# Casting ahead, products further ahead and three phases instead of four in a dense expert layer

## The chip, the cores and the metric

The kernel runs on one core of a Trainium2 chip. A core has five engines that take their instructions in order, each from its own queue: TensorE (PE; the loads of its stationary operand are listed as PEld), VectorE (DVE), ScalarE (ACT), GpSimd (POOL) and SyncE (SP), which here only issues DMAs. They work on SBUF, an on-chip memory of 128 partitions, and PE writes into PSUM. Sixteen DMA engines, which all queues share, move data between SBUF and the device's memory (HBM). The metric is device microseconds of one execution; the time before is the median of three runs.

## The reference

One layer of a decoder block on 512 tokens of width 1024: a mixing part (gated linear attention and windowed attention), then PEER, a retrieval of single-neuron experts. The second half of the time, and the whole change, lie in PEER:

```
def expert_block(args):
    xb, ib, gb = args
    u = expert_u[ib]
    h = jax.nn.gelu(jnp.einsum('lkd,ld->lk', u, xb), approximate=False)
    return jnp.einsum('lk,lkd->ld', gb * h, expert_v[ib])
```

Each token has 8 x 16 = 128 experts out of 16384, with an index `ib` and a gate `gb` for each; `expert_u` and `expert_v` are 16384 x 1024 in float32.

## The kernel before

The tokens are split. For the last 360 (`TD`) the experts are computed **densely**: all 16384, in 128 blocks of 128, with a gate matrix that is zero where an expert wasn't picked. For the first 152 the picked rows of both tables are **gathered**, and each is multiplied and added up on DVE.

*The dense part.* A **U block** b (`h_step`) multiplies 128 rows of expert_u with the tokens: 24 matmuls into a PSUM bank, a Gelu on ACT, a result of 128 x 360. A **V block** (`v_step`) multiplies the gated result with 128 rows of expert_v: 24 matmuls into eight accumulators, which take all of PSUM. So U and V blocks cannot alternate; they run in **phases** (`PHASES`): U of 72 blocks and V of the same 72, then 21 and 21, 21 and 21, 14 and 14. "U1" below is the U stretch of phase 1, and U72 is the U block 72. The result of U stays in SBUF, in the ring (tile `ring`, 21 buffers), until V needs it. In phase 0 blocks 21 to 71 do not fit: they are spilled to HBM (`hs`, from tile `hw`) and loaded back as `hr` in V (`h_load`).

*Float32 by two parts.* Every operand is split into a high part, a cast to the format that PE takes (fp32r), and a low part, the difference; three products replace one. A weight block arrives by DMA in `raw` (512 KB, 3 buffers); ACT casts `whi`, then DVE subtracts for `wlo`. `Stream.get(u)` asks for block u and at that time issues `whi` and `wlo` of block u+2 and the DMA of u+3.

*The gated product.* `w_a(b)` multiplies the result with the gate on DVE (`wr`) and casts it on ACT (`wh`); `w_b(b)` subtracts on DVE (`wl`). In V block b the code runs `w_a(b+2)`, `pump`, `w_b(b+2)`, then `v_step(b)` with its `get`, and `pump` again. `g_load` brings the gates of four blocks (tile `gt`, 720 KB) and is issued when `w_a` reaches the first of the four before. The gate matrix is built during U of phase 0 (`route`, `feed`: one-hot tiles on DVE, small matmuls on PE in between the U blocks, `gbuild`), and written to HBM as `gd`.

*The gather.* 308 steps: 128 u, 26 x, 128 v, 26 y. A u or v step handles 128 tokens, one expert each. The other 24 tokens are laid out five times, so that an x or y step has 120 rows. POOL issues indirect DMAs (tile `rows`, four at a time), DVE does one 128 x 1024 operation a step. `pump()` decides while the program is built how many steps go behind each block: it adds up estimated times of PE, DVE and the DMAs, and puts in steps as long as DVE and DMAs are less than `SLACK` ahead of PE. The order is then fixed.

*Ends of phases.* `sum_phase` moves the eight accumulators to `yT`: ACT copies them in phase 0, DVE adds them after later phases; two at once, as the next U blocks need their banks, the others behind the next blocks.

Of the kernel before, what the change touches and what calls it, by code (L numbers as in the profile page):

```python
# [9 lines left out]
F32 = mybir.dt.float32  # L10
F32R = mybir.dt.float32r
# [4 lines left out]
OP = mybir.AluOpType  # L16
# [23 lines left out]
UNITS = (["skv"] * 4 + ["glr"] + ["sq"] * 8 + ["gr"] * 8 + ["gb"] * 8  # L40
         + GH[0] + GH[1] + ["wb"] * WB[0] + GH[2] + ["wb"] * (WB[1] - WB[0]) + GH[3] + ["wb"] * (8 - WB[1])
         + ["ga"] * NGA + ["wa", "ga"] * (8 - NGA) + ["wa"] * NGA + ["wo"] * 8 + ["wpq"] * 16)


NB = 128
N0 = 72
NRING = 21
NOO = 6
AHEAD = 5
LEAD = 20  # L50
# [1 line left out]
SLACK = 3.0  # L52
DUTY = 0.92
GL = 3
WA = 2
XG = 24
XR = 128 // XG
XS = -(-128 // XR)
# [3 lines left out]
TD = T - TG  # L62
# [2 lines left out]
CQ = CT // 4  # L65


PHASES = [(0, N0)] + [(b, min(b + NRING, NB)) for b in range(N0, NB, NRING)]
DENSE = [(kind, b) for lo, hi in PHASES for kind in "UV" for b in range(lo, hi)]


@with_exitstack
def tile_block(ctx, tc, xT, wst, smalls, wgk2, keysT, uT, vv, u_rows, v_rows, out):
    nc = tc.nc
    ctx.enter_context(tc.manual_schedule())

    P = ctx.enter_context(tc.tile_pool(name="keep", bufs=1, side="left"))
# [9 lines left out]
    def S(n):  # L87
        return sm[:, SM[n][0]:SM[n][1]]
# [10 lines left out]

    class Stream:  # L100
        def __init__(self, nraw, nsp, ahead):
            self.src, self.raw, self.sp = [], {}, {}
            self.nraw, self.nsp, self.ahead = nraw, nsp, ahead
            self.nd = self.ns = 0
            self.lo_eng = lambda u: nc.gpsimd
            self.defer, self.goal = False, 0

        def dmas(self, n):
            while self.nd < min(n, len(self.src)):
                r = P.tile([128, 1024], F32, name=f"raw{self.nd}", tag="raw", bufs=self.nraw)  # L110
                nc.sync.dma_start(r, self.src[self.nd])
                self.raw[self.nd] = r
                self.nd += 1

        def splits(self, n):
            while self.ns < min(n, len(self.src)):
                u = self.ns
                self.dmas(u + 1)
                r = self.raw.pop(u)
                hi = P.tile([128, 1024], F32R, name=f"whi{u}", tag="whi", bufs=self.nsp)  # L120
                lo = P.tile([128, 1024], F32R, name=f"wlo{u}", tag="wlo", bufs=self.nsp)
                nc.scalar.copy(hi, r)  # L122
                self.lo_eng(u).tensor_tensor(lo, r, hi.bitcast(F32), OP.subtract)  # L123
# [88 lines left out]
    for kb in range(KB):  # L212
        g = S("gmix")[:, kb:kb + 1]
# [621 lines left out]
    for d in range(9):  # L835
        if d < 8:
# [5 lines left out]
            g = S("gffn")[:, d:d + 1]  # L842
# [24 lines left out]
    hr, qps = {}, {}  # L867
# [63 lines left out]
    for hp in range(17):  # L931
# [19 lines left out]
        if hp == NXU - 1:  # L951
# [3 lines left out]
            Dn = ctx.enter_context(tc.tile_pool(name="dense", bufs=1, side="right"))  # L955
# [249 lines left out]
    ring, gts, wrs, ws, accs = {}, {}, {}, {}, {}  # L1205
    later = []
# [7 lines left out]
    def spilled(b):  # L1214
        return NRING <= b < N0

    def h_step(b, each=None):
        w = get("U", b)
        bank = PS.tile([128, 512], F32, name="hp", tag=f"M{b % 2}")
        ps = proj(w, XN, n=TD, c0=TG, bank=bank, each=each)  # L1220
        if spilled(b):
            g = Dn.tile([128, TD], F32, name="hw", tag="hw", bufs=3)
        else:
            g = Dn.tile([128, TD], F32, name="ring", tag="ring", bufs=NRING)
            ring[b] = g
        nc.scalar.activation(g, ps[:, :TD], AF.Gelu)
        pe[0] += 24 * (TD / 2400 + 0.014)
        if spilled(b):
            nc.scalar.dma_start(hs[b - NRING], g)
            xfer(0.5)  # L1230
        for f in later[:2]:
            f()
        del later[:2]

    def h_load(b):
        if spilled(b):
            ring[b] = Lt.tile([128, TD], F32, name="hr", tag="hr", bufs=4)
            nc.sync.dma_start(ring[b], hs[b - NRING])
            xfer(0.5)

    def g_load(q):
        g = Lt.tile([128, NCK, 4 * CT], F32, name="gt", tag="gt", bufs=2)
        nc.sync.dma_start(g, gd[q])
        xfer(1.8)
        gts[q] = g

    def w_a(b):
        if b % 4 == 0 and b // 4 + 1 < NB // 4:
            g_load(b // 4 + 1)
        g = gts[b // 4].rearrange("p c (i t) -> p c i t", t=CT)[:, :, b % 4, :]  # L1250
        wr = Lt.tile([128, TD], F32, name="wr", tag="wr", bufs=2)
        nc.vector.tensor_tensor(wr.rearrange("p (c t) -> p c t", t=CT),  # L1252
                                ring.pop(b).rearrange("p (c t) -> p c t", t=CT), g, OP.mult)
        dve[0] += (2 * TD + 200) / 960
        hi = Lt.tile([128, TD], F32R, name="wh", tag="wh", bufs=3)
        nc.scalar.copy(hi, wr)  # L1256
        wrs[b] = (wr, hi)

    def w_b(b):
        wr, hi = wrs.pop(b)  # L1260
        lo = Lt.tile([128, TD], F32R, name="wl", tag="wl", bufs=3)
        nc.vector.tensor_tensor(lo, wr, hi.bitcast(F32), OP.subtract)  # L1262
        ws[b] = (hi, lo)

# [35 lines left out]
    def pump():  # L1300
        for x in (dve, dma):
            x[0] = max(x[0], pe[0] - SLACK)
        while side and dve[0] < pe[0] + SLACK and dma[0] < pe[0] + SLACK:
            step()

    def sum_phase(ph):
        def f(c):
            if ph:
                nc.vector.tensor_tensor(yT[:, c], yT[:, c], accs[c][:, 0:TD], OP.add)  # L1309
# [27 lines left out]
    BANKS = ("S2", "S2", "PT", "O", "M2", "M3", "M0", "M1")  # L1337
    for ph, (b0, b1) in enumerate(PHASES):
        for b in range(b0, b1):
            if b == b1 - 1:  # L1340
                for v in range(b0, b0 + WA):
                    w_a(v)
                    w_b(v)
            h_step(b, feed if LEAD <= b < N0 - TAIL else None)
            if b == RS[0]:
                dve[0] = 27.0
            for _ in range(RS.count(b)):
                next(r_)
            if b == RS[-1]:
                side.append(gather())  # L1350
            if b == N0 - TAIL - 1:
                for _ in r_:
                    pass
                late[0] = True
                step(4)
                assert early[0] == 0
                sR.close()
                Lt = ctx.enter_context(tc.tile_pool(name="late", bufs=1, side="right"))
                yT = Lt.tile([128, 8, TD], F32, name="yT")
            if b == N0 - GL:  # L1360
                g_load(0)
            if b >= RS[-1]:
                pump()
        while later:
            later.pop(0)()
        big = PS.tile([128, 2, 512], F32, name="oacc", tag="S2")
        for c, tg in enumerate(BANKS):
            accs[c] = big[:, c] if c < 2 else PS.tile([128, 512], F32, name="oa", tag=tg)
        end = b1 == NB
        for b in range(b0, b1 - 2 if end else b1):  # L1370
            h_load(b + WA + 3)
            if b + WA < b1:
                w_a(b + WA)
                pump()
                w_b(b + WA)
            v_step(b, b == b0, b == b1 - 1)
            pump()
            if b == NB - 6:
                flush()
                xr = Dn.tile([128, 4, D], F32, name="xr", tag="gbuf", bufs=2)  # L1380
                nc.sync.dma_start(xr[0:TB, 1], x1s[XG:, 1])
                nc.sync.dma_start(xr[0:XG, 0], x1s[0:XG, 1])
                nc.sync.dma_start(xr[:, 2:4], x1s[:, 2:4])
        if not end:
            sum_phase(ph)
# [92 lines left out]
```

## Time and profile before

| | |
|---|---|
| median of 3 runs | 1954.98 us (1952.24 to 1958.17) |
| the profiled execution | 1948.18 us |
| its span, first to last instruction | 1946.4 us |
| PE busy | 1791.0 us (92%) |
| DVE busy | 1399.3 us (72%) |
| ACT busy | 740.9 us (38%) |
| POOL busy | 686.2 us (35%) |
| DMA, mean over the span | 217 GB/s |

The profile is of one execution. In groups and timelines a row names line, engine, operation, written and read tiles and shapes; in brackets or behind the bar stands how long the engine was idle before and whose work ended that. "ACT whi L122" is ACT's instruction on line 122 that writes `whi`. A matmul's duration overlaps the next one's, so PE's time is read from starts. In windows, PEclk is the granted share of PE's full clock, and the DMA share can pass 1 slightly, as transfers on one engine overlap.

### The profile page before, as it was taken

The page shows a single profiled execution, that of the slowest core. Times are in us where ns is not written, and L with a number is a line of the kernel's source. Part 1 is how long each engine was busy: PE and PEld are TensorE (multiplying, and loading weights), DVE is VectorE, ACT ScalarE, POOL GpSimd, SP SyncE. Part 2 cuts the span into 40 slices and gives each one's busy share as a digit, 9 for nine tenths or more (in the row PEclk, how much of TensorE's full clock was granted, in tenths as well). Part 3 has the DMA queues.
Part 4 walks back from the last instruction along what each step waited for, and adds up shares of the span by engine and source line. Part 5 has one row for each costly group of instructions (what it writes and reads, how often), then busy time and mean ns, then how long its engine had stood idle before and what let it go on. Part 6 is the DMA issues. An engine that isn't in the chain of part 4 may idle for free.

```text
span 1946.4 us, 27062 instructions
## 1 busy us (share of the span) xinstructions
PE 1791.0 (92%) x10087; PEld 1615.4 (83%) x10087; DVE 1399.3 (72%) x2772; ACT 740.9 (38%) x1139; POOL 686.2 (35%) x492
## 2 busy tenths in 40 slices
PE   7999999999989998999998988988989879987977
PEld 5676688887868898999998888888888779976976
DVE  7557524452469967999994877777768789888666
ACT  4445423443442244666663233333323223322322
POOL 2333444445544501112331333232444335534430
PEclk9999999999989999999999999999989999999999
DMA  4221222222432335798999788888999889978995
GB/s 154 76 65 47 63 91 83 71 72 96 152 108 76 98 109 167 234 285 285 321 330 329 286 321 307 308 323 313 271 262 401 288 303 348 362 274 321 266 258 150
DMA packets 159971, 422.24 MB, mean 217 GB/s; under 512 B 15111, under 2 KB 69255, under 8 KB 159455
## 3 DMA queue, kind: packets, MB, share of 16 engines
q1 hardware_dynamic: 108143, 251.31, 38.7%
q0 software_dynamic: 44352, 159.80, 24.1%
q10 hardware_dynamic: 7344, 9.40, 1.4%
q8 instruction: 79, 1.29, 0.3%
q14 instruction: 53, 0.43, 0.1%
HBM read 383.24 MB, written 37.19 MB: 216 GB/s over the span
## 4 chain that ended last, share of the span: by engine, by line
PE 45%; DVE 23%; DMA 11%; issue 10%; ACT 7%; POOL 3%; SPq 1%; ACTq 0%; DVEq 0%; POOLq 0%
PE hp L172 16%; PE mm L172 16%; ACT whi L122 5%; DVE accv L1194 4%; DVE wlo L123 4%; PE mm L189 4%; PE gp L1076 4%; DMA raw<-in_vv_dram 4%; DVE rows L1181 3%; DMA rows<-in_v_rows_dram,misc 3%; POOL rows L1173 2%; DVE wr L1252 2%; DMA raw<-in_uT_dram 2%; DMA rows<-in_u_rows_dram,misc 2%; DVE accy L1194 1%
## 5 line engine op out<-in xcount | busy, mean ns | idle before, releaser
L122 ACT CAST whi<-raw 128x1024 fp32r<-128x1024 f32 x349 | 364.5, 1045 | 207.5 <-DMA raw<-in_uT_dram 108.6
L123 DVE TENSOR_TENSOR wlo<-raw,whi 128x1024 fp32r<-128x1024 f32 x250 | 306.6, 1226 | 120.8 <-ACT whi L122 115.3
L172 PE MATMUL hp<-xh,whi 128*128 128x360 f32 x1024 | 349.8, 342 | 19.3 <-DVE yT L1309 10.5
L172 PE MATMUL hp<-xh,wlo 128*128 128x360 f32 x1024 | 342.6, 335 | 20.7 <-DVE wlo L123 19.0
L172 PE MATMUL hp<-xl,whi 128*128 128x360 f32 x1024 | 340.9, 333 | 0.0
L123 POOL TENSOR_TENSOR wlo<-raw,whi 128x1024 fp32r<-128x1024 f32 x99 | 244.6, 2474 | 244.5 <-ACT whi L122 243.1
L1271 PE MATMUL oa<-wh,wlo 128*128 128x360 f32 x768 | 260.4, 339 | 43.9 <-DVE wlo L123 43.4
L1271 PE MATMUL oa<-wh,whi 128*128 128x360 f32 x768 | 256.4, 334 | 23.6 <-ACT whi L122 21.9
L1173 POOL DMA_INDIRECT rows<-in_v_rows_dram,misc x154 | 183.3, 1190 | 260.2 <-DVE accv L1194 179.5
L1271 PE MATMUL oa<-wl,whi 128*128 128x360 f32 x768 | 250.3, 326 | 0.0
L1173 POOL DMA_INDIRECT rows<-in_u_rows_dram,misc x110 | 134.4, 1222 | 292.1 <-DVE rows L1181 252.2
L1256 ACT CAST wh<-wr 128x360 fp32r<-128x360 f32 x128 | 63.2, 494 | 410.1 <-DVE wr L1252 400.4
L172 PEld LDWEIGHTS hp<-xh,wlo 128*128 128x128 f32 x1024 | 197.1, 192 | 24.5 <-DVE wlo L123 22.6
L172 PEld LDWEIGHTS hp<-xh,whi 128*128 128x128 f32 x1024 | 197.4, 193 | 21.0 <-issue 6.5
L1271 PEld LDWEIGHTS oa<-wh,wlo 128*128 128x128 f32 x768 | 144.4, 188 | 72.0 <-DVE wlo L123 71.4
L172 PEld LDWEIGHTS hp<-xl,whi 128*128 128x128 f32 x1024 | 197.6, 193 | 0.0
L1271 PEld LDWEIGHTS oa<-wh,whi 128*128 128x128 f32 x768 | 144.6, 188 | 38.9 <-ACT whi L122 35.2
L1194 DVE SCALAR_TENSOR_TENSOR accv<-rows,misc,accv 128x1024 f32<-128x1024 f32 x128 | 164.2, 1283 | 4.6 <-DMA rows<-in_v_rows_dram,misc 2.7
L1173 POOL DMA_INDIRECT row<-in_u_rows_dram,misc x44 | 66.7, 1517 | 264.9 <-DVE row L1181 190.9
L1271 PEld LDWEIGHTS oa<-wl,whi 128*128 128x128 f32 x768 | 144.7, 188 | 0.0
L1077 ACT COPY gbuild<-gp 128x512 f32<-128x512 f32 x90 | 99.6, 1106 | 82.5 <-PE gp L1076 81.2
L1262 DVE TENSOR_TENSOR wl<-wr,wh 128x360 fp32r<-128x360 f32 x128 | 69.5, 543 | 83.3 <-ACT wh L1256 79.5
(566 smaller groups left out, 3484.6 us busy)
## 6 DMA issues: line engine op xcount, KB each, us to landing
raw<-in_uT_dram SPq DMA_DIRECT2D x128, 512.0 KB
raw<-in_vv_dram SPq DMA_DIRECT2D x128, 512.0 KB
raw<-in_wst_dram SPq DMA_DIRECT2D x93, 512.0 KB
gd<-gbuild SPq DMA_DIRECT2D x80, 288.0 KB
gt<-gd SPq DMA_DIRECT2D x32, 720.0 KB
hs<-hw ACTq DMA_DIRECT2D x51, 180.0 KB
hr<-hs SPq DMA_DIRECT2D x51, 180.0 KB
rows<-in_v_rows_dram,misc POOLq DMA_INDIRECT x154
```

The lines of the kernel that those rows point to most:

```text
L122: nc.scalar.copy(hi, r)
L123: self.lo_eng(u).tensor_tensor(lo, r, hi.bitcast(F32), OP.subtract)
L172: nc.tensor.matmul(ps[:, :n], a[:, kb, :], b[:, kb, c0:c0 + n], start=(kb == 0 and i == 0), stop=(kb == KB - 1 and i == 2))
L189: nc.tensor.matmul(banks[t], a[:, kb, t * 128:(t + 1) * 128], b[:, k, :], start=(first and k == 0 and i == 0), stop=(last and k == kk - 1 ...
L1076: nc.tensor.matmul(p[:, k], o[:, 0, k], o[:, 1, k], start=True, stop=True)
L1077: nc.scalar.copy(gbs[c].rearrange("p i t -> p t i")[:, q * 4:q * 4 + 4, :], p)
L1173: nc.gpsimd.indirect_dma_start(out=rows[n][0:m, :], out_offset=None, in_=u_rows if kn in "ux" else v_rows, in_offset=bass.IndirectOffsetOn ...
L1181: nc.vector.scalar_tensor_tensor(cur, cur, 1.0, x_[0:m, :], OP.mult, OP.mult, accum_out=h_[0:m, s_:s_ + 1])
L1194: nc.vector.scalar_tensor_tensor(acc[0:m, :], cur, w_[0:m, s_:s_ + 1], acc[0:m, :], OP.mult, OP.add)
L1256: nc.scalar.copy(hi, wr)
L1262: nc.vector.tensor_tensor(lo, wr, hi.bitcast(F32), OP.subtract)
L1271: nc.tensor.matmul(accs[c][:, 0:TD], v_[:, cs], a, start=(first and i == 0), stop=(last and i == 2))
```

## The change

The stream of weights now casts `whi` one block further ahead than it subtracts `wlo` (`his`, `more`), with a fourth buffer of `raw` and `whi`. `wr` is made three blocks ahead (`WA`) and its `wl` one block later; the first three are made together at the end of each U stretch. `g_load` is issued one block later, with the first two before V of phase 0. Phase 0 has 82 blocks, then 23 and 23; the ring has 15 buffers and `hr` 8, and U blocks of later phases that do not fit the ring use `hr`. So blocks 15 to 81 are spilled. `sum_phase` lets ACT copy out the first two accumulators and DVE adds them later.

```
-N0 = 72
-NRING = 21
+N0 = 82
+NRING = 15
+NHR = 8
-WA = 2
+WA = 3
-PHASES = [(0, N0)] + [(b, min(b + NRING, NB)) for b in range(N0, NB, NRING)]
+PHASES = [(0, N0)] + [(b, min(b + NRING + NHR, NB)) for b in range(N0, NB, NRING + NHR)]
...
+        def tile(self, tag, dt, u, n):
+            k = u - len(UNITS)
+            if k >= 0 and k % (n + 1) == n:
+                return Dn.tile([128, 1024], dt, name=f"{tag}{u}", tag=tag + "x", bufs=1)
+            return P.tile([128, 1024], dt, name=f"{tag}{u}", tag=tag, bufs=n)
...
+        def his(self, n):
+            while self.nh < min(n, len(self.src)):
+                u = self.nh
+                self.dmas(u + 1)
+                hi = self.tile("whi", F32R, u, self.nsp)
+                nc.scalar.copy(hi, self.raw[u])
+                self.hi[u] = hi
+                self.nh += 1
...
-                self.dmas(u + 1)
-                r = self.raw.pop(u)
-                hi = P.tile([128, 1024], F32R, name=f"whi{u}", tag="whi", bufs=self.nsp)
+                self.his(u + 1)
+                r, hi = self.raw.pop(u), self.hi.pop(u)
                 lo = P.tile([128, 1024], F32R, name=f"wlo{u}", tag="wlo", bufs=self.nsp)
-                nc.scalar.copy(hi, r)
...
             self.splits(u + 1 if self.defer else self.goal)
-            self.dmas(u + self.nraw + 1)
+            if self.more:
+                self.his(self.goal + self.more)
+            self.dmas(u + self.nraw + self.more + 1)
...
+        elif b < N0 or (b - N0) % (NRING + NHR) < NRING:
+            g = ring[b] = Dn.tile([128, TD], F32, name="ring", tag="ring", bufs=NRING)
         else:
-            g = Dn.tile([128, TD], F32, name="ring", tag="ring", bufs=NRING)
-            ring[b] = g
+            g = ring[b] = Lt.tile([128, TD], F32, name="hr", tag="hr", bufs=NHR)
...
-        if b % 4 == 0 and b // 4 + 1 < NB // 4:
+        if b % 4 == 1 and 4 < b and b // 4 + 1 < NB // 4:
             g_load(b // 4 + 1)
...
-    st.lo_eng = lo_eng
+    st.lo_eng, st.more = lo_eng, 1
...
+        for c in (7, 6):
             if ph:
+                t = Lt.tile([128, TD], F32, name="ev", tag="wr", bufs=3)
+                nc.scalar.copy(t, accs[c][:, 0:TD])
+                later.append(lambda c=c, t=t: add(c, t))
...
             if b == b1 - 1:
                 for v in range(b0, b0 + WA):
                     w_a(v)
+                for v in range(b0, b0 + WA - 1):
                     w_b(v)
...
             if b == N0 - GL:
                 g_load(0)
+                g_load(1)
...
-            h_load(b + WA + 3)
+            if not ph:
+                h_load(b + NHR - 1)
             if b + WA < b1:
                 w_a(b + WA)
-                pump()
-                w_b(b + WA)
+            pump()
+            if b + WA - 1 < b1:
+                w_b(b + WA - 1)
```

The buffers of `wr`, `wh` and `wl` go from 2, 3 and 3 to 3, 5 and 4.

The order of instructions in V of phase 0, about its block 24, first on DVE before. Numbers in names tell buffers of one name apart; `wlo191` is the low part of the 191st weight block of the program.

```order
L1252 TENSOR_TENSOR wr_10319<-hr_10193,gt_10076 128x360
L1262 TENSOR_TENSOR wl_10323<-wr_10319,wh_10321 128x360
L123 TENSOR_TENSOR wlo191_10328<-raw191_10285,whi191_10327 128x1024
L1181 SCALAR_TENSOR_TENSOR rows_10068,misc_4266<-rows_10068,xtok_3904 128x1024
L1252 TENSOR_TENSOR wr_10358<-hr_10237,gt_10076 128x360
```

On ACT before, at the same place:

```order
L1256 CAST wh_10321<-wr_10319 128x360
L122 CAST whi191_10327<-raw191_10285 128x1024
L1256 CAST wh_10360<-wr_10358 128x360
L122 CAST whi192_10366<-raw192_10325 128x1024
L1256 CAST wh_10407<-wr_10405 128x360
```

DVE now:

```order
L1270 TENSOR_TENSOR wr_10749<-hr_10584,gt_10506 128x360
L1280 TENSOR_TENSOR wl_10753<-wr_10710,wh_10712 128x360
L138 TENSOR_TENSOR wlo201_10755<-raw201_10682,whi201_10718 128x1024
L1198 SCALAR_TENSOR_TENSOR rows_10498,misc_4266<-rows_10498,xtok_3904 128x1024
L1198 SCALAR_TENSOR_TENSOR rows_10661,misc_4266<-rows_10661,xtok_3904 128x1024
L1270 TENSOR_TENSOR wr_10794<-hr_10623,gt_10670 128x360
```

ACT now:

```order
L1274 CAST wh_10712<-wr_10710 128x360
L128 CAST whi201_10718<-raw201_10682 128x1024
L1274 CAST wh_10751<-wr_10749 128x360
L128 CAST whi202_10757<-raw202_10720 128x1024
L1274 CAST wh_10796<-wr_10794 128x360
```

Before, `wl_10323` reads `wh_10321`, which reads the `wr_10319` just made; now `wl_10753` reads `wh_10712` of the block before, and `wlo201` a `whi201` that stands ahead of the next `wh` on ACT.

The 120-row steps of the gather (x, which read `xtk`) on DVE before stand among U blocks of phase 1:

```order
L123 TENSOR_TENSOR wlo_12428<-raw_12390,whi_12427 128x1024
L1181 SCALAR_TENSOR_TENSOR rows,misc<-rows,xtk_3905 120x1024
L123 TENSOR_TENSOR wlo_12462<-raw_12425,whi_12461 128x1024
L1181 SCALAR_TENSOR_TENSOR rows,misc<-rows,xtk_3905 120x1024 x2
L123 TENSOR_TENSOR wlo_12502<-raw_12459,whi_12501 128x1024
```

and now among the V blocks 55 to 77 of phase 0:

```order
L1198 SCALAR_TENSOR_TENSOR rows,misc<-rows,xtk_3905 120x1024 x2
L1270 TENSOR_TENSOR wr<-hr,gt 128x360
L1280 TENSOR_TENSOR wl<-wr,wh 128x360
L138 TENSOR_TENSOR wlo_12068<-raw_11994,whi_12030 128x1024
L1198 SCALAR_TENSOR_TENSOR rows,misc<-rows,xtk_3905 120x1024
```

In the same way the y steps move from U and V of phase 3 to V107 to V122. Counted over the whole order of DVE, gather steps before are 45 in U of phase 0, 86 in its V, then 38, 31, 39, 32, 26 and 11 in the stretches that follow (the last the V of phase 3); now 68, 94, 42, 36, 41 and 27.

More of the change, by code (lines that the diff above doesn't have):

```diff
@@ L101, in __init__ @@
         def __init__(self, nraw, nsp, ahead):
-            self.src, self.raw, self.sp = [], {}, {}
+            self.src, self.raw, self.hi, self.sp = [], {}, {}, {}
             self.nraw, self.nsp, self.ahead = nraw, nsp, ahead
-            self.nd = self.ns = 0
+            self.nd = self.nh = self.ns = 0
             self.lo_eng = lambda u: nc.gpsimd
-            self.defer, self.goal = False, 0
+            self.defer, self.goal, self.more = False, 0, 0
+        def tile(self, tag, dt, u, n):
[3 more added lines that the diff above has]
+            return P.tile([128, 1024], dt, name=f"{tag}{u}", tag=tag, bufs=n)
         def dmas(self, n):
             while self.nd < min(n, len(self.src)):
-                r = P.tile([128, 1024], F32, name=f"raw{self.nd}", tag="raw", bufs=self.nraw)
+                r = self.tile("raw", F32, self.nd, self.nraw)
                 nc.sync.dma_start(r, self.src[self.nd])
@@ L1236, in h_load @@
         if spilled(b):
-            ring[b] = Lt.tile([128, TD], F32, name="hr", tag="hr", bufs=4)
+            ring[b] = Lt.tile([128, TD], F32, name="hr", tag="hr", bufs=NHR)
             nc.sync.dma_start(ring[b], hs[b - NRING])
@@ L1247, in w_a @@
     def w_a(b):
-        if b % 4 == 0 and b // 4 + 1 < NB // 4:
+        if b % 4 == 1 and 4 < b and b // 4 + 1 < NB // 4:
             g_load(b // 4 + 1)
         g = gts[b // 4].rearrange("p c (i t) -> p c i t", t=CT)[:, :, b % 4, :]
-        wr = Lt.tile([128, TD], F32, name="wr", tag="wr", bufs=2)
+        wr = Lt.tile([128, TD], F32, name="wr", tag="wr", bufs=3)
         nc.vector.tensor_tensor(wr.rearrange("p (c t) -> p c t", t=CT),
@@ L1254, in w_a @@
         dve[0] += (2 * TD + 200) / 960
-        hi = Lt.tile([128, TD], F32R, name="wh", tag="wh", bufs=3)
+        hi = Lt.tile([128, TD], F32R, name="wh", tag="wh", bufs=5)
         nc.scalar.copy(hi, wr)
@@ L1260, in w_b @@
         wr, hi = wrs.pop(b)
-        lo = Lt.tile([128, TD], F32R, name="wl", tag="wl", bufs=3)
+        lo = Lt.tile([128, TD], F32R, name="wl", tag="wl", bufs=4)
         nc.vector.tensor_tensor(lo, wr, hi.bitcast(F32), OP.subtract)
@@ L1306, in sum_phase, with add @@
     def sum_phase(ph):
-        def f(c):
+        def add(c, src):
+            nc.vector.tensor_tensor(yT[:, c], yT[:, c], src, OP.add)
+            dve[0] += 0.47
+        for c in (7, 6):
             if ph:
-                nc.vector.tensor_tensor(yT[:, c], yT[:, c], accs[c][:, 0:TD], OP.add)
-                dve[0] += 0.47
+                t = Lt.tile([128, TD], F32, name="ev", tag="wr", bufs=3)
+                nc.scalar.copy(t, accs[c][:, 0:TD])
+                later.append(lambda c=c, t=t: add(c, t))
             else:
                 nc.scalar.copy(yT[:, c], accs[c][:, 0:TD])
-        for c in (7, 6):
-            f(c)
-        later.extend([lambda c=c: f(c) for c in range(5, -1, -1)])
+        for c in range(5, -1, -1):
+            a = accs[c][:, 0:TD]
+            later.append(lambda c=c, a=a: add(c, a) if ph else nc.scalar.copy(yT[:, c], a))
     def finish(c):
@@ L1369, in tile_block @@
         end = b1 == NB
+        if not ph:
+            for b in range(NRING, NHR - 1):
+                h_load(b)
         for b in range(b0, b1 - 2 if end else b1):
-            h_load(b + WA + 3)
+            if not ph:
+                h_load(b + NHR - 1)
             if b + WA < b1:
                 w_a(b + WA)
-                pump()
-                w_b(b + WA)
+            pump()
+            if b + WA - 1 < b1:
+                w_b(b + WA - 1)
             v_step(b, b == b0, b == b1 - 1)
```

## The prediction

> **What bounds the kernel now.** The page's first lines give the span and the engines' shares. TensorE (PE) is busy 92% of the span, but that is an average over stages, so the next view is the windows, cut at the stretches of the dense part, which fills the second half.
>
> ```profile
> span 1946.4 us, 27062 instructions
> PE 1791.0 (92%) x10087; PEld 1615.4 (83%) x10087; DVE 1399.3 (72%) x2772; ACT 740.9 (38%) x1139; POOL 686.2 (35%) x492
> ```
>
> In the windows a row gives start and end, length, each engine's busy time, PE's granted clock (PEclk), the share of time that the DMA engines are busy, and what they move.
>
> ```profile
> core 0: us, PE busy (x) PEld busy (x) DVE busy (x) ACT busy (x) POOL busy (x), PEclk, DMA share, GB/s
> 744.00:1022.90 278.90, 274.91 (x1882) 274.28 (x1881) 268.71 (x608) 164.82 (x187) 66.58 (x44) 0.99 0.86 277
> 1022.90:1054.90 32.00, 23.80 (x123) 22.90 (x122) 13.09 (x19) 8.77 (x13) 8.76 (x9) 0.89 1.02 357
> 1054.90:1391.40 336.50, 303.65 (x1731) 280.72 (x1729) 253.40 (x382) 105.52 (x146) 97.63 (x81) 1.00 0.84 305
> 1391.40:1493.60 102.20, 90.11 (x504) 87.38 (x504) 72.72 (x90) 32.02 (x48) 48.10 (x41) 0.95 1.03 307
> 1493.60:1601.90 108.30, 90.17 (x504) 81.84 (x504) 86.94 (x97) 32.39 (x44) 35.38 (x33) 1.00 0.84 311
> 1601.90:1685.90 84.00, 83.97 (x505) 84.00 (x505) 74.98 (x68) 28.84 (x42) 48.12 (x40) 0.98 0.96 359
> 1685.90:1795.10 109.20, 89.69 (x506) 81.80 (x505) 88.81 (x97) 31.21 (x43) 40.93 (x33) 0.99 0.82 297
> 1795.10:1864.80 69.70, 60.50 (x337) 59.61 (x337) 48.19 (x46) 18.02 (x27) 27.73 (x24) 0.92 0.96 274
> 1864.80:1924.90 60.10, 52.82 (x288) 48.68 (x289) 43.47 (x52) 18.46 (x27) 11.23 (x8) 0.96 0.86 236
> 1924.90:1946.40 21.50, 13.95 (x78) 10.56 (x76) 11.71 (x28) 0.89 (x1) 0.00 (x0) 0.95 0.23 74
> ```
>
> The rows from 1022.9 are: the last five U blocks of phase 0 (U67 to U71), its 72 V blocks, 21 U, 21 V, 21 U, 21 V, 14 U, 12 V, and the last two V blocks with the end. A block is 24 matmuls. The row of 1601.9 shows U blocks that never wait: 21 in 84.0 us, 4.00 each. V blocks that never wait stand at the start of the first V stretch, seven of them (x168, a window of line 1271 alone):
>
> ```profile
> 1054.90:1082.44 27.54, 27.54 (x168) 27.54 (x169) 1.00 0.73 251
> ```
>
> That is 3.93 us a block. Yet the 72 V blocks take 336.5, or 4.67 each, and the two later V stretches of 21 blocks 108.3 and 109.2 (5.2 each). PE loses 336.5 - 283 = 53 us in the first and 26 and 27 us in the others. VectorE (DVE) explains it, first by its groups in the stretch 1054.9 to 1391.4:
>
> ```profile
> L1181 DVE SCALAR_TENSOR_TENSOR rows<-rows,xtok 128x1024 f32<-128x1024 f32 x83 | 98.9, 1219 | 0.0
> L123 DVE TENSOR_TENSOR wlo<-raw,whi 128x1024 fp32r<-128x1024 f32 x73 | 89.4, 1225 | 38.6 <-ACT whi L122 37.5 <-PE oacc L1271 0.8 <-issue 0.3
> L1262 DVE TENSOR_TENSOR wl<-wr,wh 128x360 fp32r<-128x360 f32 x71 | 38.5, 543 | 45.0 <-ACT wh L1256 43.7 <-issue 1.3
> ```
>
> and then by the timeline of one V block, on DVE and on ScalarE (ACT):
>
> ```profile
> 1119.41 0.53 DVE L1252 TENSOR_TENSOR wr<-ring,gt 128x360 f32<-128x360 f32 x1
> 1120.58 0.54 DVE L1262 TENSOR_TENSOR wl<-wr,wh 128x360 fp32r<-128x360 f32 x1 [0.64 <-ACT wh L1256]
> 1121.52 1.22 DVE L123 TENSOR_TENSOR wlo<-raw,whi 128x1024 fp32r<-128x1024 f32 x1 [0.41 <-ACT whi L122]
> ...
> 1120.05 0.49 ACT L1256 CAST wh<-wr 128x360 fp32r<-128x360 f32 x1 [4.10 <-DVE wr L1252]
> 1120.45 1.04 ACT L122 CAST whi<-raw 128x1024 fp32r<-128x1024 f32 x1
> ```
>
> DVE makes wr, then waits 0.64 for ACT's wh before wl, then 0.41 for ACT's whi before wlo. ACT has sat idle 4.10 us, for wr: a ring of the two engines, with 1.05 us of DVE idle a block. Over the stretch that is 38.6 + 45.0 = 83.6 us of idle beside 253.4 busy: 337.0, which is the stretch (336.5). **So V stretches are bound by DVE with its waits for ACT, not by PE.**
>
> **The change part by part.**
>
> *Casts and products ahead.* whi is cast three blocks ahead instead of two, wr three instead of two, with wl made one block after its wr. In the changed order both things that DVE waits for belong to the block before; ACT, which idles 4.10 us of every 5.5, has made them by then. The 83.6 us go. What is late next: DVE's own work, PE, or the DMAs. For 82 V blocks DVE's work is 253.4 x 82/72 = 289 us (the order gives 94 gather steps on 82 blocks, 86 on 72 before, so the same mix), PE's is 82 x 3.93 = 322. PE is next, if the DMAs follow.
>
> *The DMAs.* Sizes are in the page's list of DMA issues, rates in windows, and DVE's groups in the windows of 1380 and 1818 tell which gathers run there.
>
> ```profile
> raw<-in_vv_dram SPq DMA_DIRECT2D x128, 512.0 KB
> ...
> gt<-gd SPq DMA_DIRECT2D x32, 720.0 KB
> ...
> hr<-hs SPq DMA_DIRECT2D x51, 180.0 KB
> ```
>
> ```profile
> 1380.00:1460.00 80.00, 69.92 (x386) 67.16 (x385) 53.15 (x75) 25.42 (x40) 35.96 (x29) 0.94 1.03 258
> 1460.00:1500.00 40.00, 35.54 (x207) 34.09 (x207) 34.67 (x35) 13.69 (x20) 20.40 (x19) 1.00 1.02 400
> 1818.00:1908.00 90.00, 75.09 (x415) 70.95 (x414) 61.21 (x62) 24.40 (x36) 29.22 (x24) 0.94 1.00 259
> ```
>
> ```profile
> L1181 DVE SCALAR_TENSOR_TENSOR rows<-rows,xtk 120x1024 f32<-120x1024 f32 x25 | 30.6, 1226 | 23.8 <-DMA rows<-in_u_rows_dram,misc 23.8
> ...
> L1194 DVE SCALAR_TENSOR_TENSOR accy<-rows,misc,accy 120x1024 f32<-120x1024 f32 x23 | 29.5, 1282 | 2.7 <-DMA rows<-in_v_rows_dram,misc 2.4
> ```
>
> Full engines (share about 1) carry 400 GB/s at 1460, but 258 at 1380 and 259 at 1818. The last two rows are DVE's groups in those two stretches: there the gather runs its 120-row steps, x and y. While they are in flight everything is slow. A weight or a gather of 128 rows is 0.524 MB, a gate load 0.737, an hr load 0.184, an x or y gather 0.491.
>
> V0 to V54 of the changed phase 0 need 55 weights, 14 gate loads, 47 hr and 60 gathers: 28.8 + 10.3 + 8.6 + 31.5 = 79 MB, 198 us at 400 GB/s and 258 at the 307 that this kind of stretch shows now; PE needs 216. I take 223, near PE, because the row of 1460 shows what the engines carry when they are asked. V55 to V77 hold the 26 x steps, which today stand beside U blocks. There 23 weights, 6 gate loads, 20 hr and the x gathers are 12.1 + 4.4 + 3.7 + 12.8 = 33 MB: 90 us if PE sets the time, 128 at 258 GB/s. I take 122, near the row, a little less since some of it falls between x transfers. V78 to V81: 16. **V of phase 0: 361 us.**
>
> The Trainium skill, page "DMA: Bandwidth & Descriptors", in "Why a DMA increments its semaphore by 16 and not by 1", says that a transfer is split over the largest number of engines up to 16 that divides its rows, so 120 rows would use 15. By that rule x would lose a sixteenth, V55 to V77 would be PE's 90 us and the sum some 60 us lower (with y as well); the trace does not agree, since the rate falls by a third, and the sum stays with the trace.
>
> *Phases.* U of phase 0 gets ten blocks more: 10 x 4.00 = 40 us. The gate building beside it is the same work spread thinner; DVE there is at 268.7 of 278.9, and gets ten wlo and 23 gather steps at 1.22, so 309 of 319: tight, 1 us allowed (0 to 10). U77 thus starts at 1064. The five blocks after it cost 32.0 today (20 of work, DMAs at 1.02); with one weight more in store I take 31 (20 to 35). 16 more blocks are spilled and read back, 16 x 2 x 0.184 = 5.9 MB; the writes hide under U, where the DMAs are at 0.86, the reads are counted above.
>
> *U of phases 1 and 2.* 23 blocks, 92 us each. The first loses the x steps, which made it 102.2 for 21; both look like the row of 1601.9, where the order has 39 gather steps on 21 blocks (now 42 and 41 on 23).
>
> *V of phase 1.* DVE without its waits:
>
> ```profile
> L1194 DVE SCALAR_TENSOR_TENSOR accv<-rows,misc,accv 128x1024 f32<-128x1024 f32 x34 | 43.6, 1282 | 0.5
> ```
>
> This is from the stretch 1685.9 to 1795.1: (88.81 - 43.6)/21 = 2.15 us a block beside the gather, so 23 x 2.15 + 36 x 1.28 = 95.6 for the 36 steps of the new order, above PE's 90.4. I take 100 (90 to 119, the old pace).
>
> *First products moved, gate loads a block later, sums by ACT.* U93 waits for DVE to add out the accumulators:
>
> ```profile
> 1601.93 0.40 PE L172 MATMUL hp<-xh,whi 128*128 128x360 f32 x1 [4.17 <-DVE yT L1309]
> ...
> PE hp L172 <- DVE yT L1309: 10.5, 2, 6.3
> ```
>
> Now ACT copies the two that the next U blocks need, so the 4.17 and 6.3 become a copy of about half a microsecond; one of the two boundaries is gone with its phase. The 92 for U2 has that in it. Two gate loads together before V0 fall into the stretch priced at 31.
>
> *V of phase 2 and the end.* It holds all y steps, in V107 to V122: with the rows fetched ahead some 18 blocks, 12.8 + 9.4 + 3.3 = 25.5 MB, at 259 GB/s 98 us against PE's 71. So 21 x 3.93 + 30 = 112 (83 to 120), then the last two blocks and the end as now, 21.5.
>
> **Sum**, from the profiled execution: 1064 + 31 = 1095, + 361 = 1456, + 92 = 1548, + 100 = 1648, + 92 = 1740, + 112 = 1852, + 21.5 = 1873.5. Its own time is 1948.18 for a span of 1946.4, so 1.8 lie around it: 1875, **73 us less**. The median of the runs is 1954.98, 6.8 above the profiled one; less 72 it is **1883**.
>
> **The rivals.**
> - *The DMAs take over in V.* If mixed traffic carries no more than the 305 to 311 GB/s of today's V rows, V0 to V54 take 258 and V of phase 1 (35 MB) 113: 48 us more, 1931. For it: the share is 0.84 already, and the waits removed were DVE's. Against it: 400 at 1460.
> - *The 120-row gathers cost nothing extra*, since their slowness came from U blocks that asked for everything at once: 32 us less for x and 30 for y, 1821. Against it: 259 GB/s in 1818 to 1908, of which half are V blocks.
> - *Slower: x beside V starves DVE.* DVE takes a row step in its place in the order; if the row is late, wr, wl and wlo queue behind it, and PE behind them; already now DVE waits 23.8 us for 25 rows. From 1883 to 1961 it must lose 78 us more; that is when the 33 MB of V55 to V77 take 200 us, below 165 GB/s. It would give 1965. Against it: 258 holds with three quarters of the share on gathers.
> - *It does not do what it says.* If ACT's whi, behind a raw load that lands late, still comes last, the 1.05 us of each V block stay, and only boundaries are won: V of phase 0 at today's 4.67 is 383, with 27 for x 410 against 361, and V of phase 1 at 5.2 is 120 against 100: 69 us more, 1952.
>
> **How the numbers follow.** Forecast 0.62, by its own bounds 1858 to 1905; DMAs bound 0.15; x free 0.07; starving 0.07; nothing removed 0.09. The range 1855 to 1930 leaves out the two last, which end near or above the time before, and the free x, and reaches to the DMA case, whose size is itself an upper one. A measurement of this kernel tells about 0.3% (6 us) from no change: faster 0.87 (the first three and part of the last), same 0.05, slower 0.08.
>
> **What would show it.** In the changed profile wl and wlo of V blocks should have almost no idle for wh or whi; V blocks before the 120-row steps 4.0 to 4.1 us; the V blocks with x about 5.3, with the DMA share at 1 and near 260 GB/s, DVE then waiting for rows; U stretches at 4.0 a block; no wait of U for yT over 1 us. I am wrong if DVE's idle in V goes to rows or raw loads all through phase 0, if U of phase 0 stretches past 1100, or if x and y run at 400 GB/s.

## The result and the profile after

| | before | changed |
|---|---|---|
| median | 1953.61 us (4 runs, 1949.94 to 1958.17) | 1834.54 us (4 runs, 1830.56 to 1837.78) |
| ratio, 95% interval | | 0.9388 [0.936, 0.9417] |
| the profiled execution | 1948.18 us, span 1946.4 | 1830.56 us, span 1828.8 |

The change takes 119 us off, 6.1%. The forecast had 73, and the range, 1855 to 1930, misses the time on the fast side. One run of e1 below, in which the granted clock was 0.846 instead of 0.985, took 1976.41 us and is left out of its median. The page of the changed kernel shows PE at 96% where it was at 92%:

```profile
span 1828.8 us, 27244 instructions
PE 1754.5 (96%) x10087; PEld 1618.4 (88%) x10087; DVE 1377.6 (75%) x2764; ACT 746.6 (41%) x1141; POOL 697.8 (38%) x492
```

The windows of the changed kernel, cut at its own stretches (length, then busy time of PE, PEld, DVE, ACT and POOL, the clock, the DMA share and GB/s): U20 to U76 with the gate building, U77 to U81, V0 to V54, V55 to V77, V78 to V81, U1, V1, U2, and V of phase 2 up to V125. The row of the last two blocks and the end, 20.7 us, is left out.

```profile
744.00:1059.60 315.60, 310.47 (x2098) 310.01 (x2097) 301.78 (x652) 179.20 (x205) 102.72 (x67) 0.99 0.91 305
1059.60:1089.20 29.60, 23.23 (x123) 22.64 (x122) 13.37 (x20) 8.59 (x13) 9.11 (x8) 0.88 0.97 352
1089.20:1306.50 217.30, 217.30 (x1323) 217.30 (x1322) 184.56 (x288) 84.65 (x113) 77.52 (x60) 1.00 0.99 365
1306.50:1412.00 105.50, 96.07 (x553) 91.91 (x552) 71.74 (x112) 31.48 (x43) 24.79 (x22) 0.98 1.04 295
1412.00:1429.70 17.70, 16.81 (x98) 15.70 (x98) 17.36 (x22) 7.36 (x11) 11.85 (x8) 1.00 1.01 402
1429.70:1521.50 91.80, 91.80 (x553) 91.80 (x553) 84.75 (x74) 35.38 (x54) 51.64 (x47) 1.00 1.01 394
1521.50:1612.40 90.90, 90.90 (x554) 90.90 (x553) 89.65 (x101) 33.52 (x46) 42.54 (x35) 1.00 0.98 377
1612.40:1704.20 91.80, 91.80 (x554) 91.80 (x553) 84.74 (x80) 33.32 (x48) 52.50 (x44) 1.00 1.00 373
1704.20:1808.10 103.90, 90.79 (x506) 87.46 (x505) 73.88 (x88) 30.12 (x42) 23.89 (x21) 0.95 0.98 259
```

In V0 to V54, U1, V1 and U2 PE's busy time is the whole stretch: 3.95 us a V block, 3.99 a U block, no wait at all, with the DMA engines at 0.98 to 1.01. What is lost behind U76 lies mainly in three places: V55 to V77 and V of phase 2, where the 120-row gathers run (295 and 259 GB/s), and U77 to U81.

DVE's groups by shape in V0 to V54, and one V block there on DVE and on ACT, the views that carried the argument before:

```profile
L138 DVE TENSOR_TENSOR wlo<-raw,whi 128x1024 fp32r<-128x1024 f32 x56 | 68.6, 1226 | 31.1 <-issue 16.6 <-ACT wh L1274 12.6 <-ACT whi L128 1.9
L1280 DVE TENSOR_TENSOR wl<-wr,wh 128x360 fp32r<-128x360 f32 x56 | 29.3, 524 | 0.0
```

```profile
1187.70 0.53 DVE L1270 TENSOR_TENSOR wr<-hr,gt 128x360 f32<-128x360 f32 x1
1188.15 0.53 DVE L1280 TENSOR_TENSOR wl<-wr,wh 128x360 fp32r<-128x360 f32 x1
1188.59 1.22 DVE L138 TENSOR_TENSOR wlo<-raw,whi 128x1024 fp32r<-128x1024 f32 x1
```

```profile
1188.32 0.49 ACT L1274 CAST wh<-wr 128x360 fp32r<-128x360 f32 x1 [3.17 <-DVE wr L1270]
1188.72 1.04 ACT L128 CAST whi<-raw 128x1024 fp32r<-128x1024 f32 x1
```

wl now starts 0.45 us after wr, before ACT has begun the wh of that wr; it reads the wh of the block before. wl has no idle time at all. wlo still has 31.1 us of idle in this stretch, 0.55 a block: 1.9 is put down to whi, 12.6 to the wh ahead of it, and 16.6 to nothing that the profile shows. As PE never waits here, none of it costs time.

### The profile page after: what moved, and what is told of

The parts are those of the page before. It is cut to its first block, busy times and chain, and to the rows that moved or that the text cites. A ratio compares the mean times of both kernels' runs of the same rounds, so it can differ in the third digit from the quotient of the medians.

```text
span 1828.8 us, 27244 instructions
## 1 busy us (share of the span) xinstructions
PE 1754.5 (96%) x10087; PEld 1618.4 (88%) x10087; DVE 1377.6 (75%) x2764; ACT 746.6 (41%) x1141; POOL 697.8 (38%) x492
## 4 chain that ended last, share of the span: by engine, by line
PE 72%; DMA 11%; DVE 10%; ACT 3%; issue 2%; SPq 1%; POOL 1%; DVEq 0%; ACTq 0%; POOLq 0%
PE hp L189 26%; PE mm L189 17%; PE oa L1289 13%; DMA raw<-in_vv_dram 5%; PE mm L206 4%; PE gp L1093 4%; PE oacc L1289 4%; DMA rows<-in_v_rows_dram,misc 2%; DMA hr<-hs 2%; DMA raw<-in_uT_dram 1%; DVE wlo L138 1%; PE sc L933 1%; ACT whi L128 1%; DVE stt L413 0%; DVE accy L1211 0%
## 5 line engine op out<-in xcount | busy, mean ns | idle before, releaser
L189 PE MATMUL hp<-xh,whi 128*128 128x360 f32 x1024 | 345.7, 338 | 2.0 <-ACT hw L1244 2.0
L189 PE MATMUL hp<-xh,wlo 128*128 128x360 f32 x1024 | 337.3, 329 | 10.1 <-DVE wlo L138 10.1
L1289 PE MATMUL oa<-wh,wlo 128*128 128x360 f32 x768 | 255.3, 332 | 9.6 <-DVE wlo L138 9.2
L1289 PE MATMUL oa<-wl,whi 128*128 128x360 f32 x768 | 254.1, 331 | 7.0 <-DVE wl L1280 7.0
L1190 POOL DMA_INDIRECT row<-in_u_rows_dram,misc x67 | 102.7, 1533 | 268.7 <-DVE row L1198 192.9
L189 PEld LDWEIGHTS hp<-xh,wlo 128*128 128x128 f32 x1024 | 194.0, 189 | 10.8 <-DVE wlo L138 10.7
L189 PEld LDWEIGHTS hp<-xh,whi 128*128 128x128 f32 x1024 | 193.7, 189 | 2.6 <-ACT hw L1244 2.6
L1190 POOL DMA_INDIRECT rows<-in_u_rows_dram,misc x87 | 108.4, 1246 | 224.6 <-DVE rows L1198 188.6
L189 PEld LDWEIGHTS hp<-xl,whi 128*128 128x128 f32 x1024 | 193.8, 189 | 0.0
L189 PE MATMUL mm<-hhi,whi 128*128 128x512 f32 x264 | 107.1, 406 | 0.9 <-DVE gb L587 0.9
```

Source lines behind the costliest of these rows:

```text
L189: nc.tensor.matmul(ps[:, :n], a[:, kb, :], b[:, kb, c0:c0 + n], start=(kb == 0 and i == 0), stop=(kb == KB - 1 and i == 2))
L1190: nc.gpsimd.indirect_dma_start(out=rows[n][0:m, :], out_offset=None, in_=u_rows if kn in "ux" else v_rows, in_offset=bass.IndirectOffsetOn ...
L1289: nc.tensor.matmul(accs[c][:, 0:TD], v_[:, cs], a, start=(first and i == 0), stop=(last and i == 2))
```

## The experiments

The times of before beside these runs are 1949 to 1952 us; each ratio is against them. "The changed kernel" is 1834.5.

**e1, weights not cast ahead.** The fourth buffers of `raw` and `whi` and the step ahead go.

```
-            if k >= 0 and k % (n + 1) == n:
-                return Dn.tile([128, 1024], dt, name=f"{tag}{u}", tag=tag + "x", bufs=1)
...
-    st.lo_eng, st.more = lo_eng, 1
+    st.lo_eng, st.more = lo_eng, 0
```

> The changed kernel with the weight highs cast at the same distance as the lows again (no fourth raw and whi buffer). Theory (the ring between DVE and ACT was the cost, and the cast ahead is what opens it): whi stands on ACT behind the wh that waits for this block's wr, so wlo waits about 1.05 us a V block again; DVE then needs 2.03 + 1.05 + gather, about 4.4 us a V block in phase 0 and 5.0 in phase 1: 50 to 65 us slower than the changed kernel, 1885 to 1900. Rival (the longer phase 0 and fewer phases bring most of the gain): under 20 us slower, below 1855.

1904.1 us, ratio 0.9765 [0.9731, 0.9799]: 70 us slower than the changed kernel, a little more than the theory's range. The window of V0 to V54 and DVE's groups in it:

```profile
1098.29:1340.21 241.92, 227.77 (x1322) 215.89 (x1321) 181.50 (x281) 78.42 (x109) 69.41 (x58) 1.00 0.90 317
```

```profile
L135 DVE TENSOR_TENSOR wlo<-raw,whi 128x1024 fp32r<-128x1024 f32 x55 | 67.4, 1225 | 61.4 <-ACT whi L125 61.4
L1277 DVE TENSOR_TENSOR wl<-wr,wh 128x360 fp32r<-128x360 f32 x54 | 28.4, 526 | 0.0
```

wlo waits for whi 61.4 us in 55 blocks, 1.12 each; 181.5 busy + 61.4 idle is 242.9, the stretch (241.9). Both waits of before have moved to one place and together are about as long as they were (83.6 us in 72 blocks, 1.16 each). The edit also takes away a buffer of `raw`, but no wait of whi for a raw load shows in this stretch, so it is the cast that comes late, and not the load.

**e2, products not ahead.**

```
-WA = 3
+WA = 2
...
-            if b + WA - 1 < b1:
-                w_b(b + WA - 1)
+            if b + WA < b1:
+                w_b(b + WA)
```

(and `w_a`, `w_b` in turn for the first two products of a phase)

> The changed kernel with wr two blocks ahead and wl in the same block as its wr again. Theory: only wl's wait for wh comes back, 0.64 to 0.75 us a V block: phase 0 rises from 3.95 to about 4.1 us a block, phase 1 to about 4.7: 25 to 35 us slower than the changed kernel, 1860 to 1870. Rival (each of the two steps ahead is enough by itself, since PE has two blocks in store): under 6 us.

1851.18 us, ratio 0.9496 [0.9472, 0.9519]: 17 us slower, between theory and rival. V0 to V54:

```profile
1088.69:1305.93 217.24, 217.24 (x1322) 217.24 (x1322) 184.94 (x286) 80.41 (x111) 89.94 (x59) 1.00 0.98 358
```

```profile
L1280 DVE TENSOR_TENSOR wl<-wr,wh 128x360 fp32r<-128x360 f32 x55 | 29.3, 533 | 32.3 <-ACT wh L1274 32.3
```

The wait for wh is back, 0.59 a block, but 184.9 + 32.3 is just PE's own 217.2, so this stretch loses nothing. V1, with 1.6 gather steps a block instead of 1.1, does: 98.9 us instead of 90.9. So do V55 to V81, with 135.5 instead of 123.2; there ACT waits 46.7 us for raw loads ahead of whi, and wl waits 40.2 us for wh.

**e3, neither ahead.** Both edits together.

> Both steps ahead undone, phases, gate loads and sums as in the changed kernel. Theory: V blocks run at the pace of before (4.7 in phase 0, 5.2 in phase 1): 60 to 80 us slower than the changed kernel, 1895 to 1915, with wl and wlo waiting 0.64 and 0.41 us a block. Rival (phases bring it): 1850 or below.

1905.74 us, ratio 0.9783 [0.9758, 0.9809]: 71 us slower, and no slower than e1. V0 to V54 and its groups:

```profile
1095.53:1335.56 240.03, 227.08 (x1322) 215.87 (x1322) 186.83 (x281) 78.76 (x110) 70.92 (x58) 1.00 0.91 319
```

```profile
L135 DVE TENSOR_TENSOR wlo<-raw,whi 128x1024 fp32r<-128x1024 f32 x55 | 67.4, 1225 | 23.0 <-ACT whi L125 22.2 <-PE oacc L1286 0.8
L1277 DVE TENSOR_TENSOR wl<-wr,wh 128x360 fp32r<-128x360 f32 x54 | 28.8, 533 | 30.2 <-ACT wh L1271 30.2
```

186.8 + 53.2 is 240.0, the stretch again. So the product ahead alone is worth nothing that the runs can tell (e1 against e3, 1904.1 and 1905.7): the wait it removes reappears before wlo, since whi follows wh on ACT. The cast ahead alone is worth 55 us (e2 against e3), and the product ahead 17 on top of it.

**e4, x and y gathers of 128 rows.** The indirect DMAs fetch eight rows more, row 0 each time, into partitions that nothing reads.

```
-                    m = 128 if kn in "uv" else XP_
+                    m = 128
                     nc.gpsimd.indirect_dma_start(
```

> The changed kernel, in which the indirect DMAs of the x and y steps fetch 128 rows instead of 120 (the eight more, of row 0, are not used). Theory (the 120-row shape slows every transfer): the DMAs carry about 390 to 400 GB/s in these stretches instead of 260 to 295, V blocks 55 to 77 run at 3.95 (15 us less) and V of phase 2 loses its 20 us: 30 to 35 us faster than the changed kernel, 1800 to 1805. Rival (the stretches are slow by what is fetched or by demand): no change, 1835.

**1795.54 us**, ratio 0.921 [0.9187, 0.9233]: 39 us faster than the changed kernel. V55 to V77 and V of phase 2:

```profile
1311.40:1402.20 90.80, 90.80 (x554) 90.80 (x553) 78.25 (x121) 34.34 (x46) 35.12 (x24) 1.00 0.98 367
1692.50:1775.70 83.20, 83.20 (x507) 83.20 (x506) 75.08 (x89) 29.74 (x42) 22.69 (x21) 1.00 0.85 320
```

105.5 has become 90.8 and 103.9 has become 83.2, with PE busy all the way. The queues from 1311 to 1400, in the changed kernel and then in e4, with packets, MB, and the time that the packets took as a share of the 16 engines' span (q1 carries the loads that SP issues, q0 the gathers):

```profile
q1 hardware_dynamic: 5687, 15.54, 59.7%
q0 software_dynamic: 2894, 9.88, 43.5%
```

```profile
q1 hardware_dynamic: 6981, 20.25, 61.7%
q0 software_dynamic: 3383, 12.29, 36.2%
```

A MB of gathers took half as long again as in e4 (4.4% of that span instead of 2.9%), and a MB of the other loads a quarter longer (3.8% instead of 3.0%): the shape slows what flies beside it too. By the rule in the Trainium skill's page "DMA: Bandwidth & Descriptors", section "Why a DMA increments its semaphore by 16 and not by 1", a transfer of 120 rows would go over 15 engines. As an estimate from that rule, a sixteenth would be lost. The runs do not agree: full engines carry 258 GB/s (before) and 289 (the changed kernel) with such gathers, and 400 and 402 without. Why the shape does this no run shows.

**e5, phases of 72, 23, 23 and 10.** `N0 = 72` in the changed kernel.

> The changed kernel with a phase 0 of 72 blocks, so phases of 72, 23, 23 and 10. Theory (the steps ahead are the gain, phases are worth little once the sums are ACT's): within 15 us of the changed kernel's 1835, so 1825 to 1850. Rival (fewer phases are a large part of the gain): 1860 or more.

1835.26 us, ratio 0.9401 [0.9382, 0.942]: no difference to the changed kernel. In this order x and y stand beside U of phases 1 and 3: all U stretches together take 34 us more than in the changed kernel, all V stretches 30 less.

**e6, sums on DVE.** The first two sums of a later phase by `add(c, accs[c])` at once, without the copy `ev`.

> The changed kernel with the first two accumulators of a later phase added by DVE at once, as before. Only the boundary from V of phase 1 to U of phase 2 has this. Theory (that boundary's 4.2 and 6.3 us were DVE behind its gather steps): U105 waits 3 to 6 us for yT, 4 to 7 us slower with the slower clock after it, 1838 to 1842. Rival (DVE is now early enough by itself): under 2 us.

1837.98 us, ratio 0.9424 [0.9407, 0.944]: 3 us by the medians, with intervals that meet. The wait at U105, expected at 3 to 6 us, is 0.48:

```profile
1620.74 0.40 PE L189 MATMUL hp<-xh,whi 128*128 128x360 f32 x1 [0.48 <-DVE yT L1326]
```

With the ring of waits between DVE and ACT open, DVE reaches the sums nearly when PE needs them, as the rival has it. The expected wait did not come.

**e7, gate loads one block earlier.** `b % 4 == 0` again in `w_a`.

> The changed kernel with the gate load issued at the first of four blocks again, where it waits for the buffer that the block just before frees. Theory (SP has weights in store, so its wait reaches nobody): under 5 us. Rival (SP's queue behind the gate load holds up the weights): V blocks wait for whi once in four, 10 us or more.

1844.23 us, ratio 0.944 [0.9418, 0.9461]: 10 us slower by the medians, twice the theory's limit, though one of its five runs took 1836.03, inside the changed kernel's range. SP's waits from 1089 to 1300, of e7 and then of the changed kernel (L119 issues the weights, L1261 the gates):

```profile
SPq L119 <- DVE wlo L138: 78.0, 38, 3.9
SPq L1261 <- DVE wr L1270: 71.4, 13, 7.7
```

```profile
SPq L119 <- DVE wlo L138: 116.0, 45, 5.1
SPq L1261 <- DVE wr L1270: 14.6, 12, 2.4
```

SP stands 71 us before gate loads, up to 7.7 each, with weights behind. V0 to V54 bear it (217.3 in both). V55 to V81, with x, take 131.0 us by PE's starts instead of 123.2; but e6, which is the changed kernel up to there, takes 127.1, so half of that can be a difference between executions. That the rival is right where the DMA engines are slow is likely, and not shown.

**e8, the kernel before with 128 rows.** The edit of e4.

> The kernel before with x and y fetched as 128 rows. Theory: the slow transfers go there too: U of phase 1 falls from 102 to about 85 us and U of phase 3 from 70 to about 58, the V stretches, which DVE sets, stay: 25 to 30 us faster than before, 1920 to 1925. Rival (the shape only matters beside the loads of V): no change.

1918.65 us, ratio 0.9828 [0.9809, 0.9847]: 33 us faster than before. The U stretches of phases 1 and 3:

```profile
1392.60:1478.00 85.40, 84.15 (x506) 83.85 (x505) 72.14 (x90) 32.60 (x48) 61.54 (x41) 1.00 0.98 374
1783.40:1843.30 59.90, 58.61 (x337) 57.71 (x337) 47.93 (x46) 18.23 (x27) 26.31 (x24) 0.96 0.90 330
```

102.2 and 69.7 have become 85.4 and 59.9. The shape costs beside U as well as beside V.

**e9, neither ahead, and 72, 23, 23 and 10.** e3 with the edit of e5.

> Both steps ahead undone and phases of 72, 23, 23 and 10: of the change only the buffers, gate loads and sums stay. The question is why the kernel with neither step ahead is still 45 us faster than before, while phases alone cost nothing. Theory (where DVE sets V, every gather step that a longer phase 0 puts beside U takes 1.15 us out of V; where PE sets it, nothing): 15 to 30 us slower than 1905, so 1920 to 1935. Rival (phases are worth nothing here either): 1905.

1928.5 us, ratio 0.989 [0.9867, 0.9913]: 23 us slower than e3, where the same edit cost nothing in e5. The time is the theory's, but the stretches show another cause. U of phase 1 (23 blocks) and of phase 3 (ten blocks):

```profile
1372.22:1492.90 120.68, 98.31 (x554) 94.10 (x553) 81.95 (x100) 35.08 (x52) 61.62 (x47) 0.97 1.03 301
1810.94:1868.23 57.29, 42.68 (x241) 40.60 (x240) 38.97 (x40) 13.46 (x20) 24.27 (x20) 0.95 0.99 256
```

By the theory V would be longer than in e3. All V stretches together take 602.9 us against 619.6, 17 less, with nearly as many gather steps beside them (157 against 153). U is longer, 660.4 against 617.8, and that in the two rows above, where x and y now stand: U of phase 1 took 92.0 in e3. So the forecast was met by luck. What the edit moves is the place of the 120-row gathers; in e3 they stand beside V blocks that DVE slows anyway, which would hide a part of what they cost. That reading fits, and was not tested.

**e10, writes of the gate matrix spread.** e4, with the last eight `put`s one a block instead of all at once.

```
-        while gout:
-            gout.pop(0)()
+        gout.pop(0)()
```

(with a `gout.pop(0)()` behind each U block from 77 on and ahead of each V block, while any is left)

> The 128-row kernel with the last eight writes of the gate matrix issued one a block instead of all at once ahead of the weights of U79. Theory (U79 and U80 lose 10 us because their weights stand behind these writes on SP): U79 and U80 fall from 18.5 us together to 8 to 10, 1785 to 1790. Rival (the DMA engines are full there whatever the order): no change, 1795.

**1786.94 us**, ratio 0.9166 [0.9149, 0.9183], the fastest: 9 us below e4. SP's timeline about U79 in e4, where U77 starts at 1063.6, then in e10, where it starts at 1058.9 (L119 loads weights, L1099 writes gates):

```profile
1065.05 9.89 SPq L1099 DMA_DIRECT2D gd<-gbuild  x8
1075.35 1.92 SPq L119 DMA_DIRECT2D raw<-in_uT_dram  x1
1077.37 1.60 SPq L119 DMA_DIRECT2D raw<-in_vv_dram  x2
```

```profile
1060.33 0.36 SPq L1099 DMA_DIRECT2D gd<-gbuild  x1
1060.78 0.45 SPq L119 DMA_DIRECT2D raw<-in_uT_dram  x1
1061.29 0.81 SPq L1099 DMA_DIRECT2D gd<-gbuild  x1
1062.21 0.70 SPq L119 DMA_DIRECT2D raw<-in_vv_dram  x1
```

The weight goes out 1.9 us after the start of U77 instead of 11.7, and U77 to V0 takes 22.9 us by PE's starts where e4 took 30.6. U79 and U80 take 10.8 together instead of 18.5, a little more than the theory's 8 to 10. So the weights stood behind the writes on SP, and the rival fell.

**e11, e9 with the sums of e6.**

> As e9, with the first two sums of later phases on DVE again, so that two boundaries have them. The question is what the 22 us between e9 and before are. Theory (where DVE sets V, the sums stand behind its gather steps, 4.2 and 6.3 us in the trace of before): 6 to 12 us slower than e9, 1935 to 1941. Rival (as with both steps ahead, little): under 4 us.

1932.75 us, ratio 0.9924 [0.9898, 0.9951]: 4 us slower than e9 for two boundaries, nearer to the rival's 4 than to the theory's 6.

**e12, the kernel before with eight hr buffers.** `bufs=8` for `hr`.

> The kernel before with eight hr buffers instead of four, nothing else. In V of phase 0 SP waits 117 us in all for such a buffer, with the weights behind it. Theory (DVE sets that stretch, weights are in store): under 6 us. Rival (late weights are part of the cost): V0 to V71 fall from 336 to under 326, 10 us or more.

1945.11 us, ratio 0.9982 [0.9964, 1.0]: 0 to 7 us less, 4 by the medians, which fits the theory. V of phase 0 takes 329.4 us by PE's starts, 7 less than before, where the rival asked for 10. Of the 22 us between e9 and before, sums and hr buffers thus account for some 8 by the medians; the rest was not divided.

## Why the prediction was right in kind and too small

The mechanism was right: DVE's waits for ACT set the V stretches, they went, and PE came next. The stretches show which terms of the sum were off:

| stretch | forecast, us | measured, us |
|---|---|---|
| start of U77 | 1064 | 1059.6 |
| U77 to U81 | 31 | 29.6 |
| V0 to V54 | 223 | 217.3 |
| V55 to V77, with x | 122 | 105.5 |
| V78 to V81 | 16 | 17.7 |
| U1 | 92 | 91.8 |
| V1 | 100 | 90.9 |
| U2 | 92 | 91.8 |
| V2 up to V125, with y | 112 | 103.9 |
| the last two blocks and the end | 21.5 | 20.7 |
| span | 1873.5 | 1828.8 |

Of the 45 us, 25 are the two stretches with 120-row gathers and 9 are V1; the range ends 28 us below the forecast, so the 25 alone would not have left it, and the 34 do. **The step that failed is the pricing of the 120-row stretches, "V55 to V77 hold the 26 x steps" and "I take 122", and "112" for y: the time of the slow transfers was nearly right, but all of it was booked as the time of these blocks.** The slow stretches of the changed kernel, by the DMA rate:

```profile
1288.00:1408.00 120.00, 110.57 (x643) 106.68 (x641) 82.08 (x128) 36.47 (x50) 31.27 (x27) 0.99 1.03 289
1698.00:1796.00 98.00, 87.00 (x486) 84.22 (x485) 71.06 (x85) 28.50 (x41) 27.75 (x24) 0.95 1.03 269
```

They last 120 and 98 us, and 122 and 98 had been worked out. That is so close partly by luck: the 120 us moved 34.7 MB at 289 GB/s, where the forecast had 33 MB at about 270. But the first begins 18 us before V55, when its rows are fetched ahead, and PE lives on what is in store until V61; the loss is 105.5 - 90.8 = 15 us, not 31. For y I had allowed 18 blocks for rows fetched ahead, and it was about 21: U126 to about V123, with a loss of 21 instead of 30. e4 confirms both from the other side: without the slow shape these stretches take 90.8 and 83.2.

The prediction also expected DVE to wait for rows beside x. DVE's groups in V55 to V77:

```profile
L1198 DVE SCALAR_TENSOR_TENSOR rows<-rows,xtk 120x1024 f32<-120x1024 f32 x24 | 28.6, 1218 | 0.0
L138 DVE TENSOR_TENSOR wlo<-raw,whi 128x1024 fp32r<-128x1024 f32 x22 | 26.9, 1222 | 35.4 <-ACT whi L128 31.0 <-PE oacc L1289 2.6 <-issue 1.8
```

The rows were never late there; the weights were. wlo waited 31.0 us for whi, and from V55 to V81 ACT waited 57.0 us for raw loads. In V of phase 2 DVE did wait for rows of y, 16.5 us.

The next term is V1, 9 us. I took DVE's work from a stretch in which it waited between its instructions. Back to back they overlap, in V1 of the changed kernel:

```profile
1559.85 1.28 DVE L1211 SCALAR_TENSOR_TENSOR accv<-rows,misc,accv 128x1024 f32<-128x1024 f32 x1
1561.05 0.53 DVE L1270 TENSOR_TENSOR wr<-ring,gt 128x360 f32<-128x360 f32 x1
1561.50 0.53 DVE L1280 TENSOR_TENSOR wl<-wr,wh 128x360 fp32r<-128x360 f32 x1
1561.94 1.22 DVE L138 TENSOR_TENSOR wlo<-raw,whi 128x1024 fp32r<-128x1024 f32 x1
1563.08 1.28 DVE L1211 SCALAR_TENSOR_TENSOR accv<-rows,misc,accv 128x1024 f32<-128x1024 f32 x1
```

Each starts some 0.08 us before the one ahead of it ends, so wr, wl and wlo take 2.03 us from start to start, not 2.15, and a gather step 1.20 to 1.25 instead of 1.28. DVE is busy 89.65 of 90.9 there: it just keeps up. That is 5 of the 9 us (95.6 had been worked out); the other 4 are the allowance up to the 100 that was taken. V0 to V54 (6 us) was such an allowance too: 216 had been worked out for PE. The start of U77 (4 us) is no term that was off: e4 and e6, whose programs are the same up to there, reach it at 1063.6 and 1063.4.

Point by point: casts and products ahead, right, but the prediction treated them as one; e1 to e3 show that the cast carries them. The DMAs, right that they carry 365 to 400 GB/s in V when asked, and the rival that they would stop at 305 to 311 fell. The time measured lies nearest to the 1821 of the rival in which x and y cost nothing extra, but that rival fell: 120-row gathers are slow by themselves beside U and beside V, as e4 and e8 show. Phases, right in the sum by accident: the stretches were priced one by one, and e5 shows that 82 or 72 makes no difference to the changed kernel, as what U loses to the 120-row gathers V gains. Sums by ACT, overpriced: with both steps ahead the wait is 0.48 us even on DVE. Gate loads a block later, which the prediction priced at nothing of their own: e7 has about 10 us by the medians. The rivals of starving and of nothing removed both fell; the range missed because the slower rivals alone widened it, while the terms of the forecast, rounded up one by one, nearly all came out on the fast side.

## What to carry to other kernels

Where two engines wait for each other once a block, look for the step whose wait ends last and open the ring there. Here the product ahead alone moved the wait behind the next cast and gained nothing, the cast ahead gained 55 us. When slow transfers are fetched ahead, charge them to the blocks in which they fly, and charge only what the store does not bear. Look at the rate in windows for a stretch whose DMAs are full but slow, and at the shapes that run there.

## What the runs showed of the hardware

Indirect DMAs of 120 rows slowed the transfers in flight with them: full engines carried 258 GB/s (before) and 289 (the changed kernel), and with 128 rows 374 (e8) and 367 (e4) in these stretches. Eight rows more a transfer, read by nobody, made the changed kernel 39 us faster and the kernel before 33. Eight writes issued in a row held SP for 9.9 us ahead of the next weight (e4); one at a time between the weights they took 8 us off that stretch (e10). DVE's instructions of 0.53 and 1.22 us started 0.45 and 1.14 us apart where nothing held them.
